# Squares of a weight behind the first cast of the weight before it, on ScalarE, in the first feed-forward half of a transformer block

## The chip, the cores and the metric

The kernel runs on one core of a Trainium2 chip. The metric is the device time of one execution in microseconds (us). Times named "of the profile" come from one execution that the hardware profiler recorded; the median comes from three other executions.

## The reference

One layer with a residual trunk, input x of 1 x 2048 x 1024 in float32:

```python
u2 = rms_norm(h, norm2_w[l])
gate = jnp.einsum('bsd,df->bsf', u2, w_gate[l])
up = jnp.einsum('bsd,df->bsf', u2, w_up[l])
h = h + jnp.einsum('bsf,fd->bsd', jax.nn.silu(gate) * up, w_down[l])
```

Ahead of this stands an attention part (an input projection, four heads of differential attention, eight heads of stick-breaking attention, an output projection) which the change does not touch. The hidden width is 2816.

## The kernel before, in words

**Arithmetic.** All large products run in float16 on TensorE, each operand as a high part and a low part (the high part is a cast, the low part is the rest), so that three float16 matmuls stand for one float32 matmul. A weight is scaled by a power of two ahead of the cast. The scale comes from the squares of the weight: a column sum over its squares, its maximum, and the exponent of that. On top of that the gate, up and down products use a scheme of seven products in place of eight on 2 x 2 blocks (`quad` and `down`). One `quad` issues seven groups of 12 matmuls, of 128 x 512 each, into the PSUM tiles `pa`, `pm`, `pm`, `pd`, and again `pa`, `pm`, `pd`. `pa` and `pd` are written twice: the second group adds to the bank, once VectorE or ScalarE has read the first result out of it.

**Stages.** The feed-forward part treats the 2048 rows in two halves. Each half runs over 11 steps of 256 hidden columns. A step has three weights of 128 x 2048 float32 values: g (gate), u (up) and d (down). In the first half each weight is loaded, scaled and split by `load_ffn`, used, and its seven split blocks are written to DRAM (`split`); the second half reads the split blocks back. Every step runs `gate` and then `up`; steps are collected in pairs, and the down products of a pair run in the next even step between its `gate` and its `up`. "Odd gate" and "even gate" are the gates of odd and even steps.

**The making of one weight (first half).** `stage` (L831) lets SyncE's queue load the weight into `fst`, which has two buffers. ScalarE squares it into `sq`, one buffer: L866 for g and u, and L184 in `scale_begin` for d, with the row sums along. TensorE adds the columns up into `fsc`: eight matmuls with ones for g and u (L874), one for d (L177). VectorE takes the maximum (L875, or L178 for d) and runs a chain of small operations (L195, L170, L171, L172, L130) to the scale `c` (L199). Then `split_weight` (L207) casts the blocks into `wg`, `wu` or `wd` on ScalarE (L210: two casts of 1024 values a partition, one from the small tile `sx` of 512, and one of 1024 behind GpSimd's work) and makes the low parts on VectorE (L215). GpSimd forms the sums and differences of blocks that the seven products need (L98, `fst<-fst` and `sx<-fst`). When all readers of an `fst` buffer are done, the next weight's transfer into it starts.

**The rest of the work around it.** The outputs of the gate products are emptied by ScalarE (L946) and VectorE (L949, L953, L959, L967, L970) into `cg` tiles, silu is applied on ScalarE (L981), VectorE multiplies by the up products (L998), and the activations are cast on ScalarE (L992) with their low parts on VectorE or GpSimd (L98). The down products L1034 are gathered by VectorE (L1040), with one copy on ScalarE (L1060).

**What sets the order.** Each engine runs its instructions in order. The program is written with generators: a weight's transfer and squares are issued at one place (`begin`), its scale and casts at a later one (`end`). Between them other work is written. A scheduler then decides the final order on each engine from its own estimate of the times, keeping data dependencies; `tc.issue_after(i)` tells it to issue what stands inside behind the instruction i. During the first two steps of the first half the kernel also finishes the normalised rows of the second half (`build_x`, tiles `bx`), and at the half's start the last output projections run (`po`, `wo`).

Of the kernel before, what the change touches and what calls it, by code (L numbers as in the profile page):

```python
# [15 lines left out]
AF = mybir.ActivationFunctionType  # L16
# [43 lines left out]
def block(tc, a, out):  # L60
    nc = tc.nc
    PE, ACT, DVE, POOL, SP = nc.tensor, nc.scalar, nc.vector, nc.gpsimd, nc.sync
    top = ExitStack()
    with top:
# [8 lines left out]
        def note(e, ns):  # L73
            load[e] += ns * KW[e]

        def pick(**cost):
            e = min(cost, key=lambda k: load[k] + cost[k] * KW[k])
            load[e] += cost[e] * KW[e]
            return e
# [29 lines left out]
        def nm(s):  # L109
            uid[0] += 1  # L110
            return f"{s}{uid[0]}"

        def c1(n=1, name="c"):
            t = cp.tile([P, n], F32, name=nm(name))
            return t
# [64 lines left out]
        def scale_begin(pieces, junk=None):  # L180
            m0 = sm.tile([P, 4], F32, tag="m0", name=nm("m0"))
            for j, pc in enumerate(pieces):
                if junk is not None:
                    ACT.activation(junk, pc, AF.Square, accum_out=m0[:, j : j + 1])  # L184
                    note("A", 0.84 * int(np.prod(pc.shape[1:])) + 200)
                else:
                    DVE.tensor_reduce(m0[:, j : j + 1], pc, op=ALU.max, axis=AX.XY if len(pc.shape) > 2 else AX.X, apply_absolute_value=True)
                    note("D", 1.05 * int(np.prod(pc.shape[1:])) + 100)
            return [m0[:, j : j + 1] for j in range(len(pieces))]
# [11 lines left out]
        def weight_scale(pieces, rW, pW, pt, junk=None):  # L201
# [2 lines left out]
            scale_end(lambda m: across(m, pt, cols), rW, pW, junk is not None, sW)  # L204
            return sW

        def split_weight(hi, lo, st, n, sW, engines="P"):  # L207
            e = pick(**{k: {"A": 0.84 * n + 200, "D": 0.53 * n + 130, "P": 1.1 * n + 100}[k] for k in engines})
            if e == "A":
                ACT.mul(hi, st, sW[:])  # L210
            elif e == "D":
                DVE.tensor_scalar(hi, st, sW[:], None, op0=ALU.mult)
            else:
                POOL.tensor_scalar(hi, st, sW[:], 0.0, op0=ALU.mult, op1=ALU.add)
            DVE.scalar_tensor_tensor(lo, st, sW[:], hi, op0=ALU.mult, op1=ALU.subtract)  # L215
            note("D", 1.05 * n + 130)
# [586 lines left out]
        with ExitStack() as ph2:  # L803
# [12 lines left out]
            def pst(t):  # L816
                pst_n[0] += 1
                if pst_n[0] % 4:
                    return ps2.tile([P, 512], F32, tag="b", bufs=6, name=nm(t))
                return psj.tile([P, 512], F32, tag="pj", name=nm(t))  # L820
# [6 lines left out]
            def stage(fg, nme):  # L827
                st = fw.tile([P, 2048], F32, tag="fst", bufs=2, name=nm("fst"))
                f0 = 256 * fg
                with tc.issue_after(rows[1].ins) if (fg, nme) == (1, "u") else nullcontext():  # L830
                    d = fetch(st, f0, nme)  # L831
                if len(keep) > 1:
                    with tc.issue_after(d.ins):
                        SP.dma_start(*keep.pop(0))
                return st
# [13 lines left out]
            def load_ffn(half, fg, names, W):  # L849
                eng = "ADP" if fg == 0 else WE  # L850
                sc = scales.setdefault(fg, {})
                for nme in names:
                    if half == 1:
                        yield
                        late = nme == "d" and fg == NFG - 1
                        w16 = (fd if nme == "d" and not late else fw).tile([P, 7, 2, 512], F16, tag="wd" if nme == "d" and not late else "wgu", bufs=2, name=nm("w" + nme))
                        SP.dma_start(w16[:].rearrange("p o s n -> p (o s n)"), split[fg, "gud".index(nme)])
                        W[nme] = w16
                        continue
                    st = stage(fg, nme)  # L860
                    r, p, sW = c1(), c1(), c1()
                    sq = fw.tile([P, 2048], BF16, tag="sq", bufs=1, name=nm("sq"))
                    if nme == "d":
                        cols = scale_begin([st[:]], sq[:])
                    else:
                        ACT.activation(sq[:], st[:], AF.Square)  # L866
                        note("A", 1900)
                    yield
                    w16 = (fd if nme == "d" else fw).tile([P, 7, 2, 512], F16, tag="wd" if nme == "d" else "wgu", bufs=2, name=nm("w" + nme))
                    pt = pst("fsc")  # L870

                    def columns(m):
                        for k in range(KT):
                            PE.matmul(pt[:, :256], lhsT=ones[:], rhs=sq[:, 256 * k : 256 * k + 256], start=k == 0, stop=k == KT - 1)  # L874
                        DVE.tensor_reduce(m, pt[:, :256], op=ALU.max, axis=AX.X)  # L875

                    scale_end((lambda m: across(m, pt, cols)) if nme == "d" else columns, r[:], p[:], True, sW)
                    sc[nme] = (r, p, sW)
                    sW = sc[nme][2]
                    tte = "DP" if fg == 0 else "P"  # L880
                    sx = fw.tile([P, 512], F32, tag="sx", bufs=1, name=nm("sx"))

                    def put(o, src, n):
                        split_weight(w16[:, o : o + n, 0], w16[:, o : o + n, 1], src, 512 * n, sW, eng)

                    if nme == "d":
                        sv = st[:].rearrange("p (f h n) -> p h f n", f=2, h=2)
                        b11, b21, b12, b22 = sv[:, 0, 0], sv[:, 0, 1], sv[:, 1, 0], sv[:, 1, 1]
                        put(0, sv[:, 0], 2)
                        tt(sx[:], b22, b12, ALU.subtract, 512, tte)  # L890
                        tt(b12, b12, b11, ALU.subtract, 512, tte)
                        tt(b11, b22, b12, ALU.subtract, 512, tte)
                        tt(b21, b21, b11, ALU.subtract, 512, tte)
                        put(2, sv[:, 1], 2)
                        put(4, sv[:, 0], 2)
                        put(6, sx[:].unsqueeze(1), 1)
                    else:
                        sv = st[:].rearrange("p (d k f n) -> p d k f n", d=2, k=4, f=2)
                        xv = sx[:].rearrange("p (k n) -> p k n", k=4)
                        wv = w16[:].rearrange("p o s (k n) -> p o s k n", k=4)  # L900

                        def putk(o, src, n):
                            split_weight(wv[:, o : o + n, 0], wv[:, o : o + n, 1], src, 512 * n, sW, eng)

                        blk = lambda f, d: sv[:, d, :, f, :]
                        putk(0, sv[:, :, :, 0, :], 2)
                        tt(xv, blk(0, 0), blk(1, 0), ALU.subtract, 512, tte)
                        tt(blk(1, 0), blk(1, 0), blk(1, 1), ALU.add, 512, tte)
                        tt(blk(0, 0), blk(1, 0), blk(0, 0), ALU.subtract, 512, tte)
                        tt(blk(0, 1), blk(0, 1), blk(0, 0), ALU.subtract, 512, tte)  # L910
                        putk(2, sv[:, :, :, 1, :], 2)
                        putk(4, sv[:, :, :, 0, :], 2)
                        putk(6, xv.unsqueeze(1), 1)
                    W[nme] = w16
                    keep.append((split[fg, "gud".index(nme)], w16[:].rearrange("p o s n -> p (o s n)")))
                    if fg == NFG - 1 and nme == "d":
                        while keep:
                            SP.dma_start(*keep.pop(0))
                if half == 0 and "g" in names:
                    kg, F = c1(), c1()  # L920
                    times(kg, sc["g"][1], p_2, 2.0 ** -14)
                    times(F, sc["g"][0], r_2, 2.0 ** (21 - 37))
                    sc["kg"], sc["F"] = kg, F
                if half == 0 and "d" in names:
                    kd = c1()
                    times(kd, sc["u"][1], p_2)
                    times(kd, kd, sc["d"][1])
                    times(kd, kd, sc["kg"], 2.0 ** (39 - 14 - 22))
                    sc["kd"] = kd
                W.update({k: sc[k] for k in ("kg", "F", "kd") if k in sc})  # L930
# [297 lines left out]
```

## Time and profile before

| what | us |
|---|---|
| median of three executions | 2779.86 (2775.68 to 2783.71) |
| span of the profiled execution | 2785.0 |
| first feed-forward half in it | about 1433 to 2105 |
| second feed-forward half in it | 2105 to 2785 |
| PE busy in the span | 2489.9 |
| DVE busy in the span | 2000.8 |
| POOL busy in the span | 1445.2 |
| ACT busy in the span | 1361.8 |

PE is TensorE's matmuls, DVE is VectorE, ACT is ScalarE, POOL is GpSimd, SP is SyncE, and SPq its DMA queue. A row of a timeline gives the start in the span, the duration of the run of like instructions in us, the engine, the line of the kernel, the operation, what is written and read with the shape, and the count; in brackets stands how long the engine idled before and what released it. A row of the waits gives the waiting instruction, whom it waited for, the total, the number of waits and the longest. A row of the windows gives the stretch, its length, the busy time of each engine with the number of instructions, the granted clock of TensorE as a share of full speed, the share of DMA time, and GB/s. Numbers behind tile names are left out there. In the listings of the order a tile's number is kept, and a row tells line, operation, output and inputs.

### The profile page before, as it was taken

The page shows a single profiled execution, that of the slowest core. Times are in us where ns is not written, and L with a number is a line of the kernel's source. Part 1 is how long each engine was busy: PE and PEld are TensorE (multiplying, and loading weights), DVE is VectorE, ACT ScalarE, POOL GpSimd, SP SyncE. Part 2 cuts the span into 40 slices and gives each one's busy share as a digit, 9 for nine tenths or more (in the row PEclk, how much of TensorE's full clock was granted, in tenths as well). Part 3 has the DMA queues.
Part 4 walks back from the last instruction along what each step waited for, and adds up shares of the span by engine and source line. Part 5 has one row for each costly group of instructions (what it writes and reads, how often), then busy time and mean ns, then how long its engine had stood idle before and what let it go on. Part 6 is the DMA issues. An engine that isn't in the chain of part 4 may idle for free. (4 is left out here: it accounts for less than half of the span.)

```text
span 2785.0 us, 45469 instructions
## 1 busy us (share of the span) xinstructions
PE 2489.9 (89%) x17084; PEld 1409.0 (51%) x17084; DVE 2000.8 (72%) x3782; ACT 1361.8 (49%) x2543; POOL 1445.2 (52%) x1008
## 2 busy tenths in 40 slices
PE   6998989888878786888889798989999999999998
PEld 4665556555545453557775343444444444444443
DVE  6888879687989989876756877777786644434445
ACT  4665656466878788765644534443442212111121
POOL 2567767665544555546665656565654332322323
PEclk9999999999999897999999999999999999999999
DMA  6788787789999998997796565655658844635534
GB/s 225 199 167 184 147 188 163 164 174 205 198 205 198 192 182 160 190 198 205 197 309 253 184 235 189 221 187 191 240 170 299 327 155 178 227 125 190 211 129 166
DMA packets 649133, 551.91 MB, mean 198 GB/s; under 512 B 506624, under 2 KB 574208, under 8 KB 638672
## 3 DMA queue, kind: packets, MB, share of 16 engines
q1 hardware_dynamic: 647088, 546.92, 71.2%
q8 instruction: 134, 2.20, 0.3%
q0 software_dynamic: 512, 1.36, 0.2%
q10 hardware_dynamic: 1312, 0.72, 0.1%
q14 instruction: 87, 0.71, 0.1%
HBM read 265.27 MB, written 151.52 MB: 150 GB/s over the span
## 5 line engine op out<-in xcount | busy, mean ns | idle before, releaser
L98 POOL TENSOR_TENSOR s<-z,s 128x1024 f16<-128x1024 f32 (+7 forms) x288 | 474.1, 1654 | 334.8 <-ACT s L89 299.3
L320 PE MATMUL pj<-w,xt 128*128 128x384 f16 x3072 | 572.3, 334 | 32.6 <-DVE st L330 11.6
L320 PEld LDWEIGHTS <-xt 128*128 128x128 f16 x3072 | 299.9, 100 | 241.8 <-issue 36.3
L448 PE MATMUL sc<-kT,qT 128*128 128x512 f16 (+3 forms) x1280 | 346.9, 362 | 74.6 <-DVE z L558 34.4
L1034 PE MATMUL pd<-wd,act 128*128 128x512 f16 x1848 | 406.2, 379 | 3.3 <-DVE hs L1040 2.4
L557 DVE TENSOR_TENSOR_SCAN z<-z,sc 128x512 f32<-128x512 f32 (+3 forms) x320 | 355.5, 1112 | 68.6 <-ACT sc L555 65.1
L458 PE MATMUL yp<-v,aT 128*128 128x64 f16 (+1 forms) x4896 | 281.2, 207 | 80.0 <-DMA aT<-s 79.2
L458 PEld LDWEIGHTS <-aT 128*128 128x128 f16 x4896 | 245.2, 102 | 169.4 <-DMA aT<-s 105.1
L936 PEld LDWEIGHTS <-wg 128*128 128x128 f16 x1848 | 183.9, 100 | 264.3 <-issue 58.8
L98 POOL TENSOR_TENSOR hs<-hs,cu 128x512 f32<-128x512 f32 x132 | 170.5, 1297 | 238.2 <-DVE cu L1040 82.6
L936 PEld LDWEIGHTS <-wu 128*128 128x128 f16 x1848 | 181.0, 98 | 222.1 <-issue 9.0
L1034 PEld LDWEIGHTS <-act 128*128 128x128 f16 x1848 | 180.6, 98 | 222.6 <-issue 4.7
L98 POOL TENSOR_TENSOR act<-cg,act 128x512 f16<-128x512 f32 x117 | 160.8, 1385 | 247.7 <-ACT act L992 141.5
L98 POOL TENSOR_TENSOR fst<-fst 128x512 f32<-128x512 f32 x97 | 179.6, 1852 | 167.6 <-DVE wd L215 78.6
L1040 DVE SCALAR_TENSOR_TENSOR hs<-pd,c,hs 128x512 f32<-128x512 f32 x192 | 142.1, 748 | 160.8 <-PE pd L1034 159.1
L89 ACT CAST s<-z 128x384 f16<-128x384 f32 (+7 forms) x216 | 170.1, 788 | 151.5 <-DMA aT<-s 56.4
L554 ACT ACTIVATE z<-sc,c 128x512 f32<-128x512 f32 (+3 forms) x320 | 202.6, 633 | 10.6 <-PE sc L448 6.5
L558 DVE TENSOR_TENSOR z<-sc,z 128x512 f32<-128x512 f32 (+3 forms) x320 | 193.3, 606 | 8.1
L992 ACT CAST act<-cg 128x512 f16<-128x512 f32 x132 | 80.6, 617 | 234.2 <-DVE cg L998 190.9
L555 ACT ACTIVATE sc<-sc,c 128x512 f32<-128x512 f32 (+3 forms) x320 | 194.8, 609 | 0.0
L761 PE MATMUL po<-wo,mt 128*128 128x256 f16 x1536 | 181.3, 276 | 11.0 <-DVE xf L764 6.3
L936 PE MATMUL pm<-X,wg 128*128 128x512 f16 x792 | 179.1, 379 | 1.2 <-ACT bx L1109 1.2
(233 smaller groups left out, 4028.4 us busy)
## 6 DMA issues: line engine op xcount, KB each, us to landing
xt<-xs SPq DMA_DIRECT2D x112, 512.0 KB, 4.4
hs<-hd SPq DMA_DIRECT2D x96, 512.0 KB, 4.3
hd<-hs SPq DMA_DIRECT2D x80, 512.0 KB, 3.2
split<-wg SPq DMA_DIRECT2D x11, 1792.0 KB, 10.5
split<-wu SPq DMA_DIRECT2D x11, 1792.0 KB, 10.3
split<-wd SPq DMA_DIRECT2D x11, 1792.0 KB, 10.4
wg<-split SPq DMA_DIRECT2D x11, 1792.0 KB, 7.3
wd<-split SPq DMA_DIRECT2D x11, 1792.0 KB, 8.4
```

Source lines behind the costliest of these rows:

```text
L89: ACT.copy(dst, src)
L98: (DVE if e == "D" else POOL).tensor_tensor(dst, a_, b_, op)
L320: PE.matmul(pj[:, :384], lhsT=xv[:, xi, kt, :], rhs=G["w"][:, wi, kt, :], start=n == 0, stop=n == 23)
L448: PE.matmul(sc[:, : 128 * w].rearrange("p (t n) -> p t n", n=P), lhsT=G["q"][i // 4][:, 2 - 2 * o + m, i % 4, :], rhs=G["k"][q][:, m, 0:w, ...
L458: PE.matmul(yp[:, y0 : y0 + wd], lhsT=aT[:, a_, :], rhs=v[:, v_ : v_ + wd], start=start and j == 0 and q == 0, stop=stop and j == nb - 1 a ...
L554: ACT.activation(om[:, lo:hi], sc[:, :w], AF.Sigmoid, scale=G["nkz"][:])
L555: ACT.activation(sc[:, :w], sc[:, :w], AF.Sigmoid, scale=G["kz"][:])
L557: DVE.tensor_tensor_scan(ov, ov, sc[:, :w], om[:, hi : hi + 1], op0=ALU.mult, op1=ALU.bypass)
L558: DVE.tensor_tensor(be[:, lo:hi], sc[:, :w], om[:, lo + 1 : hi + 1], ALU.mult)
L761: PE.matmul(po[:, sl], lhsT=mt[:, kt, P * xi : P * xi + P], rhs=wos[2 * h + n][wi][:, kt, :], start=q == 0, stop=q == 23)
L936: PE.matmul(ps_[:].rearrange("p (t n) -> p t n", n=P), lhsT=wv[:, wo, wi, 128 * kt : 128 * kt + 128], rhs=X[xo][:, :, xi, kt, :], start=st ...
L1034: PE.matmul(po[:], lhsT=act[:, ao, xi, 128 * j : 128 * j + 128], rhs=W["d"][:, wo, wi, :], start=start and u == 0 and q == 0, stop=u == nu ...
```

## The change

The ScalarE casts of a weight are kept in a list, which is emptied ahead of the next weight's casts. The squares of a weight are issued behind the first cast in the list, that is, behind the first ScalarE cast of the weight made before it. Nothing else is changed.

```diff
+        casts = []
+
+        def behind(k):
+            return tc.issue_after(casts[min(k, len(casts) - 1)].ins) if casts else nullcontext()
+
         def split_weight(hi, lo, st, n, sW, engines="P"):
             e = pick(**{k: {"A": 0.84 * n + 200, "D": 0.53 * n + 130, "P": 1.1 * n + 100}[k] for k in engines})
             if e == "A":
-                ACT.mul(hi, st, sW[:])
+                casts.append(ACT.mul(hi, st, sW[:]))
...
                     sq = fw.tile([P, 2048], BF16, tag="sq", bufs=1, name=nm("sq"))
-                    if nme == "d":
-                        cols = scale_begin([st[:]], sq[:])
-                    else:
-                        ACT.activation(sq[:], st[:], AF.Square)
-                        note("A", 1900)
+                    with behind(0):
+                        if nme == "d":
+                            cols = scale_begin([st[:]], sq[:])
+                        else:
+                            ACT.activation(sq[:], st[:], AF.Square)
+                            note("A", 1900)
...
                     sW = sc[nme][2]
                     tte = "DP" if fg == 0 else "P"
+                    casts.clear()
```

The scheduler decides the order of all engines anew under this condition. The two listings that differ most are shown at their places in the prediction.

## The prediction

> **What bounds the kernel now.** I read the page first, then the busy time by stage, then TensorE's waits in the stage that changes, then the timeline of one pair of steps there. From the page, the profiled time:
>
> ```profile
> span 2785.0 us, 45469 instructions
> ```
>
> The busy time by stage (PE's first, with its count, and the granted clock after the engines), two pairs of steps of the first feed-forward half and the whole second half:
>
> ```profile
> 1741.00:1869.00 128.00, 117.36 (x545) 54.19 (x543) 93.49 (x133) 52.85 (x62) 74.71 (x48) 0.96 0.58 201
> 1869.00:1997.00 128.00, 119.42 (x555) 55.10 (x553) 96.68 (x141) 55.50 (x65) 76.05 (x49) 0.97 0.59 205
> ...
> 2105.00:2785.00 680.00, 668.61 (x3094) 302.25 (x3091) 320.71 (x428) 119.90 (x188) 217.51 (x169) 1.00 0.54 201
> ```
>
> TensorE carries both halves. The second makes no weights and leaves nothing to gain; in the first TensorE misses 9 to 11 us in 128. Its waits in the first half (us in total, times, longest):
>
> ```profile
> PE pd L936 <- DVE cg L959: 30.4, 8, 5.9
> PE fsc L874 <- ACT sq L866: 9.2, 6, 2.4
> PE pa L936 <- ACT cg L946: 6.4, 2, 3.3
> ```
>
> One pair of steps on TensorE:
>
> ```profile
> 1799.37 4.44 PE L936 MATMUL pd<-X,wg 128*128 128x512 f16 x12 [3.47 <-DVE cg L959]
> 1803.64 0.71 PE L874 MATMUL fsc<-sq,ones 128*128 128x256 bf16 x5
> ...
> 1811.95 0.38 PE L177 MATMUL fsc<-id,m 128*128 128x128 f32 x2
> 1812.17 2.75 PE L936 MATMUL pd<-X,wu 128*128 128x512 f16 x12
> ...
> 1827.81 1.03 PE L874 MATMUL fsc<-sq,ones 128*128 128x256 bf16 x8 [1.26 <-ACT sq L866]
> ...
> 1847.25 4.73 PE L936 MATMUL pd<-X,wg 128*128 128x512 f16 x12 [5.89 <-DVE cg L959]
> ```
>
> Three holes: A, in the odd gate; B, where the even gate needs the column sums of u; C, late in the even gate, where VectorE has not emptied a bank. Behind A and C the twelve matmuls last 4.4 to 4.7 instead of 2.75 us. Why VectorE is late at C is seen some 35 us earlier. ScalarE, then VectorE:
>
> ```profile
> 1807.75 1.91 ACT L184 ACTIVATE sq<-fst 128x2048 bf16<-128x2048 f32 x1 [5.26 <-DMA fst<-in_w_down_dram]
> ...
> 1809.66 0.71 ACT L981 ACTIVATE cg<-cg,c 128x512 f32<-128x512 f32 x1
> 1810.28 2.17 ACT L210 ACTIVATE wg<-fst,c 128x1024 f16<-128x1024 f32 x2
> 1812.35 0.71 ACT L210 ACTIVATE wg<-sx,c 128x512 f16<-128x512 f32 x1
> ...
> 1825.85 1.91 ACT L866 ACTIVATE sq<-fst 128x2048 bf16<-128x2048 f32 x1 [1.07 <-DMA fst<-in_w_up_dram]
> ```
>
> ```profile
> 1805.65 0.15 DVE L199 TENSOR_SCALAR c<-c 128x1 f32<-128x1 f32 x1
> ...
> 1811.44 2.48 DVE L215 SCALAR_TENSOR_TENSOR wg<-fst,c,wg 128x1024 f16<-128x1024 f32 x2 [5.52 <-ACT wg L210]
> ...
> 1831.66 2.17 DVE L215 SCALAR_TENSOR_TENSOR wd<-fst,c,wd 128x1024 f16<-128x1024 f32 x1
> ...
> 1846.52 0.68 DVE L959 TENSOR_TENSOR cg<-pd,cg 128x512 f32<-128x512 f32 x1
> ```
>
> The scale of g is there at 1805.80, yet its casts start at 1810.28: in front of them on ScalarE stand d's squares, which wait for d's weight, and a silu behind those. VectorE, which makes the low parts, idles 5.52 us, then has work without a long wait until 1846.52. u's buffer is the one that g frees, so u's transfer, u's squares and hole B hang on the same delay.
>
> **The change: d's squares.** No instruction is added or removed. ScalarE at that place, before (sq_22378 are d's squares, wg_22338 the casts of g, cg silus, cu the up product):
>
> ```order
> L981 ACTIVATE cg_22269<-cg_22269,c_21901 128x512
> L184 ACTIVATE sq_22378,m_22379<-fst_22372 128x2048
> L981 ACTIVATE cg_22240<-cg_22240,c_21901 128x512
> L210 ACTIVATE wg_22338<-fst_22271,c_22276 128x2x512 x2
> L210 ACTIVATE wg_22338<-sx_22355,c_22276 128x512
> L946 COPY cu_22395<-pa_22382 128x512
> ```
>
> and with the change (line numbers stand 5 to 7 higher):
>
> ```order
> L988 ACTIVATE cg_22269<-cg_22269,c_21901 128x512
> L988 ACTIVATE cg_22240<-cg_22240,c_21901 128x512
> L215 ACTIVATE wg_22338<-fst_22271,c_22276 128x2x512 x2
> L215 ACTIVATE wg_22338<-sx_22355,c_22276 128x512
> L184 ACTIVATE sq_22378,m_22379<-fst_22372 128x2048
> L953 COPY cu_22395<-pa_22382 128x512
> ```
>
> The squares moved behind three casts. The casts can start at about 1805.9, 4.4 us earlier. VectorE's low parts, GpSimd's subtractions that follow them, the release of g's buffer and so u's transfer move with them, and C's add comes at about 1842.1. u's squares, 4.4 earlier, are done at 1823.4 against 1827.8: hole B closes. d's squares start at 1805.9 + 2.17 + 0.71, about 1808.7 (their data were there at 1807.75), and end 1810.7; TensorE asks for their maximum at 1811.95. Cover 1.3 us, cost 0. (In the middle pairs like that of 1966 the new order puts this matmul one product later on TensorE, with more cover.) The third cast of g keeps waiting for GpSimd's subtractions, only earlier, and d's and u's casts follow suit.
>
> **Hole A.** VectorE there, before, and then with the change (cg the odd gate, wu_22197 the odd u's low parts, act an activation's):
>
> ```order
> L949 TENSOR_TENSOR cg_22240<-pm_22242,cg_22240 128x512
> L98 TENSOR_TENSOR act_22040<-cg_21672,act_22040 128x512
> L215 SCALAR_TENSOR_TENSOR wu_22197<-fst_22112,c_22117,wu_22197 128x2x512
> L953 TENSOR_TENSOR cg_22269<-pm_22256,cg_22240 128x512
> L215 SCALAR_TENSOR_TENSOR wu_22197<-fst_22112,c_22117,wu_22197 128x2x512
> L215 SCALAR_TENSOR_TENSOR wu_22197<-sx_22214,c_22117,wu_22197 128x512
> L964 TENSOR_TENSOR cg_22292<-pd_22279,cg_22269 128x512
> ```
>
> ```order
> L98 TENSOR_TENSOR act_22040<-cg_21672,act_22040 128x512
> L956 TENSOR_TENSOR cg_22240<-pm_22242,cg_22240 128x512
> L220 SCALAR_TENSOR_TENSOR wu_22197<-fst_22112,c_22117,wu_22197 128x2x512 x2
> L960 TENSOR_TENSOR cg_22269<-pm_22256,cg_22240 128x512
> L220 SCALAR_TENSOR_TENSOR wu_22197<-sx_22214,c_22117,wu_22197 128x512
> L966 TENSOR_TENSOR cg_22292<-pd_22279,cg_22269 128x512
> ```
>
> The same set stands ahead of the last add, so A stays. One add now runs behind the wait for `act` instead of ahead of it: between 0 and one add (0.68), I take 0.3. Besides, all eight column sums of g now run behind the gate's `pd`, where before three ran ahead of it in the hole: 1.03 less 0.71, 0.3. A costs 0.6 a pair, and delays g's scale by as much.
>
> **The squares elsewhere.** In the odd step, u's squares go behind d's casts, and in the down products d's go behind the next g's:
>
> ```profile
> 1869.13 1.91 ACT L184 ACTIVATE sq<-fst 128x2048 bf16<-128x2048 f32 x1 [8.01 <-PE fsc L874]
> ...
> 1887.50 1.91 ACT L866 ACTIVATE sq<-fst 128x2048 bf16<-128x2048 f32 x1 [8.25 <-DMA fst<-in_w_up_dram]
> ...
> 1898.14 2.19 ACT L210 ACTIVATE wd<-fst,c 128x1024 f16<-128x1024 f32 x2 [6.41 <-DVE c L199]
> ```
>
> ```profile
> 1896.07 0.39 PE L177 MATMUL fsc<-id,m 128*128 128x128 f32 x2
> ...
> 1906.65 1.04 PE L874 MATMUL fsc<-sq,ones 128*128 128x256 bf16 x8
> ```
>
> u's squares would end at 1898.14 + 2.19 + 0.71 + 1.91, about 1902.9, and their sums are taken at 1906.65: cost 0, 3.7 us of cover. d's squares, now at 1869.13, move by the 2.9 us of three casts, and TensorE takes their maximum at 1896.07: cost 0; the down products' own copy on ScalarE (L1060) behind them comes at most the 1.4 us later that a scale needs from its sums (1804.35 to 1805.80), less than the one product that TensorE has in hand there: cost 0. Should a cover fail, each us beyond it is one us of TensorE.
>
> **First and last pair.** Other holes, on TensorE, and the ScalarE rows of the first pair:
>
> ```profile
> 1454.86 2.78 PE L761 MATMUL po<-wo,mt 128*128 128x256 f16 x24 [1.76 <-DVE wo L764]
> ...
> 1555.81 0.49 PE L177 MATMUL fsc<-id,m 128*128 128x128 f32 x2 [1.99 <-ACT sq L184]
> ...
> 1573.36 1.03 PE L874 MATMUL fsc<-sq,ones 128*128 128x256 bf16 x8 [1.76 <-ACT sq L866]
> ...
> 1593.21 5.28 PE L936 MATMUL pd<-X,wg 128*128 128x512 f16 x12 [5.01 <-DVE cg L959]
> ...
> 1713.99 4.44 PE L936 MATMUL pa<-X,wg 128*128 128x512 f16 x12 [3.26 <-ACT cg L946]
> ...
> 1966.79 4.44 PE L936 MATMUL pa<-X,wg 128*128 128x512 f16 x12 [3.18 <-ACT cg L946]
> ...
> 2079.88 1.03 PE L874 MATMUL fsc<-sq,ones 128*128 128x256 bf16 x8 [1.20 <-ACT sq L866]
> ...
> 2097.67 4.12 PE L936 MATMUL pd<-X,wg 128*128 128x512 f16 x12 [4.45 <-DVE cg L959]
> ```
>
> ```profile
> 1553.77 1.89 ACT L184 ACTIVATE sq<-fst 128x2048 bf16<-128x2048 f32 x1
> ...
> 1555.66 2.17 ACT L210 ACTIVATE wg<-fst,c 128x1024 f16<-128x1024 f32 x2
> ```
>
> In the first pair d's squares ran at once, so the casts gain only 1.9 us, and TensorE waits 2.9 us more for the maximum of d (1.99 now), which the 1.76 of B and C's 5.01 take up. I take 2.5, between 0 and 6. In the last pair the new order puts three low parts ahead of C's add; I take 2, between 0 (all of the 4.4 lost) and 4.4. At the start u's squares go behind two casts of g, about 1.8 us, while TensorE projects outputs (half of 2.17 and 0.71); the hole at 1454.86 and smaller ones take up most: a cost of 0.5, between 0 and 1.8.
>
> **Sum.** Three full middle pairs at 4.4 - 0.6 = 3.8: 11.4. First 2.5, last 2, start -0.5: 15.4, call it 15. The span goes from 2785.0 to about 2770. That execution is 5 us above the median shown, 2779.86, so the forecast on the median is 2765. About 0.3%, 8 us, is what a measurement here can tell from nothing.
>
> **Rivals.** *More gain.* C's wait shrinks from 5.89 to 5.89 + 1.26 - 4.4, about 2.8 us. Whether the twelve matmuls behind it stay slow is open:
>
> ```profile
> 1672.43 2.75 PE L936 MATMUL pd<-X,wg 128*128 128x512 f16 x12 [2.65 <-DVE cg L959]
> ```
>
> ```profile
> 1672.40:1675.20 2.80, 2.77 (x14) 1.34 (x14) 1.09 (x1) 2.27 (x3) 2.72 (x3) 1.00 0.00 0
> ...
> 1847.20:1852.00 4.80, 4.75 (x13) 1.72 (x13) 2.36 (x2) 2.05 (x4) 2.88 (x2) 0.57 0.40 73
> ```
>
> A wait of 2.65 left the clock at 1.00; 3.26 and 5.89 cost it (4.44 and 4.73, clock 0.57 in the latter). If all five C holes end below, 2.53 + 1.7 + 2.0 + 1.7 + 1.4 us are saved besides, 9: 2756. The Trainium skill (TensorE: Matmul & The Clock Gate, Part 1) halves the clock after an idle window of about 3.4 us that runs freely; by that limit alone all shortened C holes would stay at full clock. The trace agrees only in kind: a hole of 3.26 was already slow. Chance 0.1.
>
> *No change.* The gain is lost on VectorE. Two low parts of g take 2.48 together now, while one of d takes 2.17. If moving them puts GpSimd beside all three of g's, each costs 0.9 more, 2.7 a pair, and with A's 0.6 the pairs keep 1.1: 3 in the middle, 2 at the ends, 2775. The Trainium skill (SBUF — State Buffer, section SBUF: two separate sides) has such an operation fully block, not slow down in part. Against: GpSimd's work on g starts only behind g's first low part, so the block moves as a whole. Chance 0.2, with the lesser losses of this sign.
>
> *Slower.* d's squares behind the casts come too late for TensorE, which stops in order at their maximum. It decides at 1.3 us: if g's casts start more than that behind 1805.9. If they started as late as now, the squares would end at about 1815.2 and TensorE wait 3.2 us; at three pairs that is 10, with A's 3 and the start, 14: 2794. Against: the silus and the scale ahead of the casts are done by 1805.9 in the trace. That the order of a schedule differs from what I replay by hand is the main doubt. Chance 0.12.
>
> **Numbers.** Forecast as summed 0.58, more 0.1, no change 0.2, slower 0.12. Faster by over 0.3%: 0.68. The range goes from somewhat past the larger gain, 2753, to the upper edge of no change, 2779, and leaves out the slower case.
>
> **What would show it.** Right: VectorE's 5.5 us idle before g's low parts shrinks below 2; the six waits of the column sums for u's squares (9.2) nearly vanish; `pd` for `cg` L966 falls from 30.4 to about 22; A keeps its 3 us. Wrong: a wait of `fsc` L177 for the squares of d at every even gate, or C's waits unchanged with longer low parts.

## The result

| kernel | median us | ratio to before, 95% interval |
|---|---|---|
| before | 2781.78 (2775.68 to 2784.83, 4 runs) | |
| with the change | 2755.95 (2754.82 to 2757.25, 4 runs) | 0.991 (0.9894 to 0.9926) |
| with the change, built and timed again (the last experiment) | 2759.37 (2754.36 to 2764.57, 5 runs) | 0.9918 (0.9904 to 0.9933) |

The change saves 21 to 26 us, each median against the kernel before on the same chip (2781.78, and 2780.83 for the second timing). The forecast was 15 us, 2765 in a range from 2753 to 2779. The change is faster and the time inside the range, but the gain is 1.4 to 1.7 times the forecast, close to the price that the prediction had given to its rival of a larger gain (2756).

### The profile after

TensorE's waits in the first feed-forward half, after, in the view that was shown of before (line numbers are 7 higher here, 5 in the weight's helper):

```profile
span 2754.1 us, 45485 instructions
```

```profile
PE pd L943 <- DVE cg L966: 23.1, 9, 4.4
PE fsc L177 <- ACT sq L184: 7.0, 2, 6.7
PE fsc L880 <- ACT sq L872: 3.0, 2, 2.3
...
PE pa L943 <- ACT cg L953: 1.7, 2, 1.6
```

The total of the whole list falls from 63 to 42 us. The wait for the column sums of u and g went from 9.2 to 3.0, `pd` for `cg` from 30.4 to 23.1, and `pa` for ScalarE's copy from 6.4 to 1.7. One wait grew by more than 0.2 us, from 2.5 to 7.0: that for the maximum of d, nearly all of it at one place in the first pair.

The same pair of steps as in the prediction, after:

```profile
1778.47 2.75 PE L943 MATMUL pd<-X,wg 128*128 128x512 f16 x12 [1.62 <-DVE cg L966]
1781.05 1.04 PE L880 MATMUL fsc<-sq,ones 128*128 128x256 bf16 x8
...
1790.15 0.49 PE L177 MATMUL fsc<-id,m 128*128 128x128 f32 x2 [0.29 <-ACT sq L184]
...
1803.21 1.04 PE L880 MATMUL fsc<-sq,ones 128*128 128x256 bf16 x8
...
1822.27 5.28 PE L943 MATMUL pd<-X,wg 128*128 128x512 f16 x12 [4.42 <-DVE cg L966]
```

A fell from 3.47 to 1.62 us and has fast matmuls behind it, B is closed, and C fell from 5.89 only to 4.42. ScalarE, then VectorE, where the casts of g start:

```profile
1783.99 2.19 ACT L215 ACTIVATE wg<-fst,c 128x1024 f16<-128x1024 f32 x2 [0.59 <-issue]
1786.09 0.71 ACT L215 ACTIVATE wg<-sx,c 128x512 f16<-128x512 f32 x1
1788.10 1.91 ACT L184 ACTIVATE sq<-fst 128x2048 bf16<-128x2048 f32 x1 [1.30 <-DMA fst<-in_w_down_dram]
...
1790.01 0.56 ACT L953 COPY cu<-pa 128x512 f32<-128x512 f32 x1
```

```profile
1783.76 0.15 DVE L199 TENSOR_SCALAR c<-c 128x1 f32<-128x1 f32 x1
...
1785.18 2.48 DVE L220 SCALAR_TENSOR_TENSOR wg<-fst,c,wg 128x1024 f16<-128x1024 f32 x2 [1.14 <-ACT wg L215]
...
1790.61 0.69 DVE L956 TENSOR_TENSOR cu<-pm,cu 128x512 f32<-128x512 f32 x1 [1.27 <-ACT cu L953]
```

The casts start as soon as the scale is there, and VectorE's 5.52 us of idle time are 1.14. But d's squares still wait for their transfer, now with ScalarE's copy of the up product queued behind them, and VectorE waits 1.27 us for that copy. That is a new wait; the experiment with d and g below shows that it is the main part of what C did not lose.

### Where the 30.9 us between the two profiled spans are

The two profiles are apart before the changed part begins. An issue on SyncE's queue just ahead of it, in the kernel before, with the change, and with the change in a second profile:

```profile
1425.71 0.87 SPq L766 DMA_DIRECT2D hd<-xf  x1
```

```profile
1419.36 0.86 SPq L771 DMA_DIRECT2D hd<-xf  x1
```

```profile
1427.89 0.87 SPq L771 DMA_DIRECT2D hd<-xf  x1
```

Up to there all three have the same instruction lists. Two profiles of one and the same kernel differ by 8.5 us, so the 6 us here are scatter between executions and are no part of the change. Hence the times below are taken inside the first half, from the first matmul of the up product of step 0 to that of step 10:

| kernel | step 0 to 10, us | first pair | pairs at steps 4, 6, 8 | last pair |
|---|---|---|---|---|
| before | 638.7 | 135.5 | 126.3, 127.7, 125.1 | 124.0 |
| with the change | 614.5 | 131.2 | 118.6, 122.2, 120.4 | 122.1 |
| with the change, second profile | 613.0 | 129.9 | 118.6, 122.1, 120.4 | 122.0 |

24 and 26 us, about what the medians say: 4 to 6 in the first pair, 7.7, 5.5 and 4.7 in the middle pairs (a pair is named by its even step), 2 in the last. From step 10 to the end both spans last 648.8 us, so nothing of the change lies there.

### The profile page after: what moved, and what is told of

It is laid out like the page before. It is cut to its first block, busy times and chain, and to the rows that moved or that the text cites. A ratio compares the mean times of both kernels' runs of the same rounds, so it can differ in the third digit from the quotient of the medians.

```text
span 2754.1 us, 45485 instructions
## 1 busy us (share of the span) xinstructions
PE 2491.4 (90%) x17084; PEld 1411.9 (51%) x17084; DVE 1997.4 (73%) x3782; ACT 1361.3 (49%) x2543; POOL 1447.6 (53%) x1008
## 5 line engine op out<-in xcount | busy, mean ns | idle before, releaser
L98 POOL TENSOR_TENSOR act<-cg,act 128x512 f16<-128x512 f32 x117 | 166.6, 1437 | 231.4 <-ACT act L999 125.1
## 6 DMA issues: line engine op xcount, KB each, us to landing
split<-wg SPq DMA_DIRECT2D x11, 1792.0 KB, 11.4
split<-wd SPq DMA_DIRECT2D x11, 1792.0 KB, 10.5
```

Source lines behind the costliest of these rows:

```text
L98: (DVE if e == "D" else POOL).tensor_tensor(dst, a_, b_, op)
```

## The experiments

The theories in the expectations: theory 1 is the prediction's (d's squares delay g's casts, and so VectorE). Theory 2 came from the two profiles: g's squares, which stood ahead of ScalarE's copy and casts in the odd gate, were what made A long. All kernels start from the changed kernel. A third buffer for the weights, which would take the wait for the transfer away by itself, was not tried.

| run | median us | ratio to before, 95% interval | steps 0 to 10, us |
|---|---|---|---|
| d alone | 2761.38 | 0.9925 (0.9910 to 0.9940) | 616.8 |
| g alone | 2773.95 | 0.9971 (0.9960 to 0.9983) | 626.0 |
| u alone | 2784.07 | 1.0006 (0.9994 to 1.0018) | 640.8 |
| all but the d of step 1 | 2765.53 | 0.9937 (0.9922 to 0.9953) | 618.8 |
| all but that d and the u of step 2 | 2764.28 | 0.9936 (0.9924 to 0.9949) | 619.4 |
| d of odd steps alone | 2761.80 | 0.9926 (0.9915 to 0.9938) | 616.3 |
| all, low parts of activations on GpSimd | 2753.16 | 0.9899 (0.9883 to 0.9915) | 611.9 |
| all, VectorE slowed ahead of C | 2764.48 | 0.9934 (0.9922 to 0.9947) | 617.6 |
| d and g | 2762.85 | 0.9926 (0.9911 to 0.9941) | 616.0 |
| all, block sums shared with GpSimd | 2776.81 | 0.9978 (0.9967 to 0.9989) | 629.1 |
| d and g, low parts on GpSimd | 2754.50 | 0.9892 (0.9873 to 0.9912) | 611.8 |

### One weight's squares at a time

```diff
-                    with behind(0):
+                    with behind(0) if nme == "d" else nullcontext():
```

> Only d's squares go behind the casts of the weight before; g's and u's squares stay where they were. Theory 1 (the prediction's: the gain comes from d's squares letting VectorE start g's low parts 4.4 us earlier in the even gates): nearly all of the 26 us of the full change, 22 to 27, so 2755 to 2760 beside a kernel before at about 2781; the holes A in the odd gate stay as they were with the full change. Theory 2 (from the two traces: g's squares standing ahead of ScalarE's copy and casts were what made A as long as it was): 15 to 20 us, so 2761 to 2767, with VectorE's idle before g's low parts gone but A at 2.6 to 3.5 us again.

Measured: 21 us faster, between the two forecasts of the gain (22 to 27 and 15 to 20); the interval, 17 to 25 us, does not tell them apart. The holes do: A is 2.66, 3.50, 2.98 and 2.75 us at steps 4 to 10, as before the change and as theory 2 has it, not as with the full change. So d's squares bring most of the gain and leave A alone. VectorE's waits for g's casts behind 1600 us, before and with d alone (us, times, longest), show the mechanism:

```profile
DVE wg L215 <- ACT wg L210: 27.4, 11, 7.6
```

```profile
DVE wg L220 <- ACT wg L215: 6.5, 7, 1.1
```

And the holes A and C of the pair at step 6, with d alone:

```profile
1790.05 4.16 PE L943 MATMUL pd<-X,wg 128*128 128x512 f16 x12 [3.50 <-DVE cg L966]
1833.40 4.44 PE L943 MATMUL pd<-X,wg 128*128 128x512 f16 x12 [3.03 <-DVE cg L966]
```

A stays at 3.5, B is gone, and C falls from 5.89 to 3.03, near the 2.8 us that the prediction had for it.

```diff
+                    with behind(0) if nme == "g" else nullcontext():
```

> Only g's squares go behind the casts of the weight before. Theory 1: no gain or a loss of up to 3 us (0.6 a pair): 2781 to 2784. Theory 2: the holes A fall to about 1.5 us in two of the five pairs and by 0.2 to 0.4 in two more, with one slow group of matmuls (1.7 us) gone: 4 to 9 us, so 2772 to 2777, while VectorE still idles about 5 us before g's low parts and C stays.

Measured: 9 us faster, as theory 2 says. VectorE's wait for g's casts stays (27.1 us in 11 waits), and A shrinks to 1.26 and 1.39 us at steps 4 and 6; at steps 8 and 10 it hardly moves (2.88 and 2.90). At step 6, with g alone:

```profile
1787.39 2.75 PE L943 MATMUL pd<-X,wg 128*128 128x512 f16 x12 [1.39 <-DVE cg L966]
...
1835.39 3.09 PE L943 MATMUL pd<-X,wg 128*128 128x512 f16 x9 [3.13 <-DVE cg L966]
```

Theory 2 missed one thing: C at step 6 did not stay, it fell from 5.89 to 3.13 us. But B grew there from 1.26 to 2.29, and a wait of 1.52 us for a scale is new, so the time went to other holes, and the fall of C alone is no sign of d's squares. The reason for the shorter A is visible in the rows of before. ScalarE, then VectorE, ahead of A:

```profile
1787.77 1.91 ACT L866 ACTIVATE sq<-fst 128x2048 bf16<-128x2048 f32 x1 [1.04 <-DMA fst<-in_w_gate_dram]
1789.59 0.57 ACT L946 COPY cg<-pa 128x512 f32<-128x512 f32 x1
```

```profile
1789.22 0.15 DVE L199 TENSOR_SCALAR c<-c 128x1 f32<-128x1 f32 x1
1790.18 0.69 DVE L949 TENSOR_TENSOR cg<-pm,cg 128x512 f32<-128x512 f32 x1 [0.82 <-ACT cg L946]
1791.74 0.71 DVE L98 TENSOR_TENSOR act<-cg,act 128x512 f16<-128x512 f32 x1 [0.87 <-ACT act L992]
1792.79 1.76 DVE L215 SCALAR_TENSOR_TENSOR wu<-fst,c,wu 128x1024 f16<-128x1024 f32 x1 [0.34 <-ACT wu L210]
...
1798.63 0.68 DVE L959 TENSOR_TENSOR cg<-pd,cg 128x512 f32<-128x512 f32 x1
```

and after, VectorE at the same place:

```profile
1771.68 0.14 DVE L199 TENSOR_SCALAR c<-c 128x1 f32<-128x1 f32 x1
1772.26 0.88 DVE L98 TENSOR_TENSOR act<-cg,act 128x512 f16<-128x512 f32 x1 [0.43 <-ACT act L999]
...
1773.66 2.46 DVE L220 SCALAR_TENSOR_TENSOR wu<-fst,c,wu 128x1024 f16<-128x1024 f32 x2
...
1776.65 1.16 DVE L220 SCALAR_TENSOR_TENSOR wu<-sx,c,wu 128x512 f16<-128x512 f32 x1
1777.73 0.68 DVE L966 TENSOR_TENSOR cg<-pd,cg 128x512 f32<-128x512 f32 x1
```

Before, g's squares waited for their transfer and held up the copy and the casts behind them, and VectorE idled 0.82 + 0.87 + 0.34 us. After, 0.43. The low parts took 1.76, 1.97 and 1.75 us before and 2.46 for two and 1.16 for the third after. From the scale to A's last add it is 9.4 us before (1789.22 to 1798.63) and 6.05 after: 3.4 us less.

```diff
+                    with behind(0) if nme == "u" else nullcontext():
```

> Only u's squares go behind the casts of the weight before. Theories 1 and 2 agree: these squares have 3.7 us of cover in the odd steps and stand behind their own transfer in the even ones: within 2 us of the kernel before, about 2780. A rival (u's squares are what closes hole B) would have B's waits of 1.2 to 2.4 us gone and 6 to 9 us gained.

Measured: no difference. With u alone the column sums still wait 10.5 us in seven places, while with d alone, where u's squares were not moved, B is gone in all pairs from step 4 on. What moves with d is u's transfer: counted from the start of the up product of step 5, it is issued after 15.1 us before, 15.0 with u alone and 10.7 with d alone. So B closes through the earlier transfer of u, not through the place of its squares.

### d and g together

```diff
+                    with behind(0) if nme != "u" else nullcontext():
```

> The full change without u: d's and g's squares go behind the casts, u's stay. d alone gave 21.3 us, g alone 8.7, u alone -1.4 (within its interval of nothing). Theory 2 with parts that add up: 28 to 30 us faster than the kernel before, 2752 to 2755, the same as the full change (25.8) within 3. Rival (u's squares are needed once the others move): 2762 or slower, as both kernels that kept some of u's or d's squares in the first pair.

Measured: 20 us faster, so the parts do not add up (21 and 9 alone), and the time cannot be told apart from that of d alone, nor from the full change. The pair at step 6, with d and g:

```profile
1784.61 2.75 PE L943 MATMUL pd<-X,wg 128*128 128x512 f16 x12 [1.40 <-DVE cg L966]
...
1828.43 5.28 PE L943 MATMUL pd<-X,wg 128*128 128x512 f16 x12 [4.49 <-DVE cg L966]
```

Against d alone, A is 2.1 us shorter and its matmuls are 1.4 faster, but C is 1.5 longer and its matmuls 0.8 slower. Where C's 1.5 us come from stands on ScalarE and VectorE behind g's casts, with d alone and then with d and g; the last row of each is C's add:

```profile
1798.99 1.89 ACT L184 ACTIVATE sq<-fst 128x2048 bf16<-128x2048 f32 x1
...
1801.55 0.68 DVE L956 TENSOR_TENSOR cu<-pm,cu 128x512 f32<-128x512 f32 x1
...
1832.67 0.68 DVE L966 TENSOR_TENSOR cg<-pd,cg 128x512 f32<-128x512 f32 x1
```

```profile
1794.19 1.91 ACT L184 ACTIVATE sq<-fst 128x2048 bf16<-128x2048 f32 x1 [1.25 <-DMA fst<-in_w_down_dram]
...
1796.70 0.69 DVE L956 TENSOR_TENSOR cu<-pm,cu 128x512 f32<-128x512 f32 x1 [1.22 <-ACT cu L953]
...
1827.70 0.68 DVE L966 TENSOR_TENSOR cg<-pd,cg 128x512 f32<-128x512 f32 x1
```

Counted from the start of the up product of step 5 (1794.59 and 1788.07), TensorE is ready for C after 35.8 and 35.9 us, but VectorE's first add of the up product starts after 7.0 and 8.6, and C's add after 38.1 and 39.6. A shorter A brings all of this forward, except d's transfer: it was issued 2.7 us ahead of that start with d alone and 0.5 with d and g. So d's squares wait for it, ScalarE's copy waits behind them, and VectorE behind the copy. Theory 2 explains A, and A is worth little once d's squares are moved. That u's squares are needed once the others move, as the rival says, is not shown, though the time is the rival's: the pairs of d and g and of the full change differ clearly only at step 4 (120.4 and 118.6 us), where the matmuls behind C are slow in one and fast in the other, and with all low parts of activations on GpSimd steps 0 to 10 take 611.8 us without u and 611.9 with it.

### Down products, first pair

```diff
+                    with behind(0) if nme == "d" and fg % 2 else nullcontext():
```

> Only the squares of d of odd steps go behind g's casts; these are the ones that stand in an even gate. The d's of even steps, in the down products, stay where they were, and so do g's and u's squares. Theory 1 and 2 agree, and the prediction's zero for the down products: the same as when all d's move, 2761 within 3 us. Rival (the d's in the down products bring part of it): 2765 to 2772.

Measured: 2761.80 beside 2761.38. The zero for d's squares in the down products holds.

```diff
+                    with behind(0) if (fg, nme) != (1, "d") else nullcontext():
```

> The full change, but the squares of the d of step 1 (first pair) stay where they were. With the full change TensorE waits 6.66 us for the maximum of this d, 1.99 before, and the next twelve matmuls take 5.23 instead of 2.75 us. Theory 2: that wait falls back to about 2 and the slow group goes, 7 us, of which the later waits (C of this pair, 1.29 now, 5.01 before; B) take back 4 to 5: 2 to 3 us faster than the full change, about 2753. Rival: C takes all of it back, since g's casts start behind the squares again, and the time is 2756 to 2758.

Measured: steps 0 to 10 take 4 to 6 us longer than with the full change. TensorE's wait for that maximum did fall, from 6.66 to 1.76, but C of that pair, with the change and without this one move, is

```profile
1583.99 2.75 PE L943 MATMUL pd<-X,wg 128*128 128x512 f16 x12 [1.29 <-DVE cg L966]
```

```profile
1585.06 5.28 PE L943 MATMUL pd<-X,wg 128*128 128x512 f16 x12 [5.70 <-DVE cg L966]
```

The rival was right and too mild: C took 4.4 of the 4.9 us back, the slow matmuls behind the one hole now stand behind the other, and two smaller waits (1.64 for the up product, 1.21 at B) are new. The hole at the maximum of d had not been a loss of its own; it stood in for C.

```diff
+                    with behind(0) if (fg, nme) not in ((1, "d"), (2, "u")) else nullcontext():
```

> The full change, but in the first pair the squares of d (step 1) and of u (step 2) stay where they were. In the traces the first pair lasts 135.5 us before, 131.2 with the full change, 133.5 with the full change but for that d, and 128.3 when only g's squares move. Theory 2 (each square's move is priced by the holes around it, pair by pair): the first pair as with g alone, the rest as with the full change: 131.2 - 128.3, about 3 us faster than the full change, 2751 to 2754. Rival (the orders of neighbouring pairs hang together, so that pairs can't be added): 2756 or slower.

Measured: 2764.28, no better, with the same 5.70 us at C. In the run with g alone, C of that pair is 2.81 us; the scheduler had set VectorE's list there in another order. The rival holds: pairs cannot be put together from kernels whose lists were decided apart.

### VectorE's list ahead of the holes

```diff
-LE, SE, AE = "DP", "D", "P"
+LE, SE, AE = "P", "D", "P"
```

> The full change, and all low parts of activations on GpSimd (before 15 of the 77 in each half or so on VectorE, one of them right ahead of the last add of hole A). Theory 2 (A and C end when VectorE's list is worked off): A falls by the 0.9 to 1.2 us of that low part in the pairs, and the two A holes of 2.7 us that were followed by slow matmuls end below, 1.7 us more each: 5 to 9 us faster than the full change, 2747 to 2751. Rival (GpSimd, with the weight's subtractions queued behind more work, becomes the bound of the third casts): 2756 or slower.

Measured: 2753.16, ratio 0.9899, beside 0.991 and 0.9918 of the full change: perhaps 3 us, within the intervals, and not the 5 to 9 that theory 2 had. A at step 8 did fall from 2.68 to 2.05, yet its matmuls stayed slow, and at step 4 A rose from 1.45 to 2.06.

```diff
+                if tag == "cg" and now[0] == 0 and now[1] % 2 == 0 and now[1]:
+                    for _ in range(2):
+                        DVE.tensor_tensor(u3[:], u3[:], u3[:], ALU.max)
                 c22 = cst()
```

> The full change, with two more VectorE operations (maximum of a tile with itself, 0.6 us each, no change to the values) ahead of hole C's last add in the five even gates of the first half. If C is bound by VectorE at all five: 5 times 1.2, 6 us, and two C holes (2.44 and 2.65 now, at full clock behind them) grow beyond 3 us, which in every row so far cost 1.4 to 1.9 us more: 9 us in all, 2763 to 2767. If C were bound by something else (ScalarE's copy, GpSimd): 2756 to 2759. If the clock did not hang on the hole's length: 2762.

Measured: 2764.48, at the forecast for a C bound by VectorE. All five C holes grew, by 6.2 us together: that of step 4 from 2.44 to 3.43 us, that of step 8 from 2.65 to 3.63, that of step 6 from 4.42 to 5.75. Steps 0 to 10 grew by only 3 to 5 us, in part since the matmuls behind two A holes of 2.69 us, slow with the full change, were fast here. The part on the clock half fell: the two C holes that were to grow beyond 3 us are

```profile
1706.29 4.19 PE L943 MATMUL pd<-X,wg 128*128 128x512 f16 x12 [3.43 <-DVE cg L971]
```

```profile
1949.89 2.75 PE L943 MATMUL pd<-X,wg 128*128 128x512 f16 x12 [3.63 <-DVE cg L971]
```

the shorter with slow matmuls behind it, the longer with fast ones.

```diff
-LE, SE, AE = "DP", "D", "P"
+LE, SE, AE = "DP", "DP", "P"
```

> The full change, and the sums of activation blocks (always on VectorE) may go to GpSimd where it has less work: 11 of them move, of about 1.3 us each on VectorE. Theory 2 (the remaining C holes, 1.3 to 4.4 us, last as long as VectorE's list): those in the first half fall by up to 1.3 us each, 3 to 6 us faster than the full change. Rival (GpSimd's longer chain, or the clock behind holes of 2 to 3 us, takes it back): 2754 to 2760.

Measured: steps 0 to 10 take 15 to 16 us longer than with the full change. The balance of the kernel's own costs gave the sums to GpSimd and, in return, three activation low parts to VectorE, in a row right ahead of A's last add:

```profile
1791.62 3.63 DVE L98 TENSOR_TENSOR act<-cg,act 128x512 f16<-128x512 f32 x3
1795.17 0.68 DVE L966 TENSOR_TENSOR cg<-pd,cg 128x512 f32<-128x512 f32 x1
```

A at step 6 is 4.50 us there, 1.62 with the full change. So it did not test what it was meant to (a shorter list), only that what stands right ahead of that add counts.

```diff
-LE, SE, AE = "DP", "D", "P"
+LE, SE, AE = "P", "D", "P"
...
+                    with behind(0) if nme != "u" else nullcontext():
```

> d's and g's squares moved, u's not, and all low parts of activations on GpSimd. If parts add up: the gain of d and g (28 to 30) and the 3 us of the low parts: 2749 to 2752, the fastest kernel here. Rival: 2753 or slower, since the holes that shrink stay between 1.9 and 3.1 us, where the matmuls behind them were slow about every second time.

Measured: 2754.50, ratio 0.9892, at the rival's forecast. It is the lowest ratio of the study, but its interval (0.9873 to 0.9912) holds the ratio of all squares with the low parts on GpSimd (0.9899) and the first of the full change (0.9910). A kernel that beats the changed one was not shown.

### The full change a second time

> The full change once more, unaltered, for a second profiled execution of the same instruction lists. In the ten profiles so far the matmuls behind a hole were at full clock below 1.9 us, slow above 4, and either in between. If between 1.9 and 3.1 us it is chance (where the hole falls in a window of its own), the holes have the same lengths within 0.1 us, but of the four of 2.4 to 2.7 us (two slow in the first profile) another set is slow; if it is fixed by the work around the hole, the same two are slow. The 5.5 us by which the first profile was ahead of that of the kernel before by 1425 us, where both have the same lists, is scatter if it differs here by over 2 us. Time: 2754 to 2759.

Measured: 2759.37. From the pair at step 4 on the holes are the same within 0.1 us; in the first pair three differ (2.40 and 0.72, 2.31 and 3.14, and 6.66 and 4.13 for the maximum of d). The lead of the first profile ahead of the changed part was scatter. A and C at step 8 in both profiles, first and second:

```profile
1901.74 4.44 PE L943 MATMUL pd<-X,wg 128*128 128x512 f16 x12 [2.68 <-DVE cg L966]
...
1945.24 2.75 PE L943 MATMUL pd<-X,wg 128*128 128x512 f16 x12 [2.65 <-DVE cg L966]
```

```profile
1910.56 4.44 PE L943 MATMUL pd<-X,wg 128*128 128x512 f16 x12 [2.69 <-DVE cg L966]
...
1954.05 2.75 PE L943 MATMUL pd<-X,wg 128*128 128x512 f16 x12 [2.64 <-DVE cg L966]
```

A is slow and C fast in both. So it is with the other two of the four holes of 2.4 to 2.7 us, A at step 10 (2.69 and 2.68, slow) and C at step 4 (2.44, fast). That speaks for the work around a hole and against chance, in two executions.

## Why the prediction came out as it did

**d's squares: right, and the main term.** They alone give 21 of the 21 to 26 us. VectorE's idle time went as forecast (5.52 to 1.14), u's transfer came 4.4 us earlier with d alone, B closed.

**The sum: inside its range in part by luck, since its terms were wrong.** What TensorE lost less in the three middle pairs (at steps 4, 6 and 8), in us against before, worked out from the same rows in each profile:

| | forecast | d alone | g alone | d and g | full change |
|---|---|---|---|---|---|
| holes B and C | 13.2 | 9.6 | 0.8 | 6.6 | 7.0 |
| hole A (forecast with its column sums) | -1.8 | 0.0 | 3.6 | 3.6 | 3.4 |
| other waits | 0 | 2.4 | -1.4 | 2.2 | 2.1 |
| busy time | 0 | 3.1 | 2.8 | 3.3 | 5.3 |
| all | 11.4 | 15.2 | 5.9 | 15.7 | 17.8 |

The main term, 4.4 us a pair in B and C, was half as large in the full change. It was taken over from the pair at step 6, where d alone gives 4.1; at steps 4 and 8 it gives 2.9 and 2.7, since C there was a wait of `pa` for ScalarE's copy before and is one of `pd` for VectorE after. What made up for it the prediction had at nothing: at step 4, waits of TensorE for d's and the up product's values (0.51, 0.69 and 1.21 us before) went as well; and of the busy time, 4.4 us are faster matmuls behind A and C, 1.7 of them at C of step 4 and 1.7 at C of step 8.

**A: wrong in sign.** "The same set stands ahead of the last add, so A stays" counted VectorE's instructions, and not its waits between them, 2 us of which were for ScalarE's copy and casts behind g's squares, nor how long the low parts take at their new place. (The last row of the prediction's first listing there is L959 in the kernel before.) A fell by 1.2, 1.9, 0.4 and 0.2 us at steps 4, 6, 8 and 10. But the experiment with d and g shows that most of that comes back at C.

**d's squares' cover of 1.3 us: just used up.** TensorE waits 0.29 us at step 6. The squares end later than replayed since their transfer, not the casts, is what they wait for. The copy that is queued behind them, which the prediction quoted as the row below without pricing it, makes VectorE wait 1.27 us. With d alone neither of the two waits is there and C is 3.03 us; with d and g both are, and C is 4.49. So this chain accounts for C at step 6 being 4.42 and not 2.8; no run moved the copy alone.

**First pair, last pair, start.** Forecast 2.5, 2 and -0.5; measured 4.3 and 5.6 in two profiles, 2, and nothing that can be told. The wait for the maximum of d was put at 1.99 + 2.9, and is 6.66 and 4.13 in two profiles. At the start the holes between the output projections shrank (1.76, 1.13, 0.91 and 0.50 before; 1.20, 0.67 and 0.70 after, one of them now at the column sums), but from one and the same matmul there to the up product of step 0 it is 72.4 us before, and 71.2 and 73.0 in two profiles after.

**The rivals.** More gain: the total is what it named, 2756, and only partly for its reason. The slow groups behind holes in the half cost about 15 us before and 11 to 12 after, so the clock gave 3 to 4 us, not 9, and the waits the rest. No change through longer low parts: the three of g took 1.28, 1.28 and 1.76 us at step 6, as before, and only the fourth grew, from 1.28 to 1.91. Slower through d's squares: it happens in the first pair, where the wait grew by up to 4.7 us, and C's fall from 5.01 to 1.29 pays for most of it.

## What to carry to other kernels

An engine that works in order should not have an instruction that waits for a transfer ahead of work whose inputs are there: look at what idles downstream of it, here VectorE 35 us ahead of TensorE's hole. Holes that are ends of one engine's list are not separate gains, so price them together; shortening one moves time to the next, and taking one away by hand can cost more than it was. And count the waits inside a list, not only its instructions.

## What the hardware showed

In 14 profiles, the 157 holes of at least 1 us ahead of gate and up matmuls in the first half were followed by slow matmuls (12 in 4.0 to 5.3 us instead of 2.75) as follows: under 1.9 us 1 of 37, from 1.9 to 3.1 us 43 of 72, from 3.1 to 4 us 27 of 29, above 4 us all 19. The granted clock behind the hole of 4.42 us is 0.50, that behind the one of 2.65 us 1.00:

```profile
1822.30:1827.30 5.00, 5.00 (x12) 1.74 (x12) 2.35 (x2) 2.02 (x3) 2.79 (x2) 0.50 0.41 96
1945.30:1948.00 2.70, 2.70 (x13) 1.21 (x13) 2.32 (x2) 1.63 (x3) 2.62 (x2) 1.00 0.00 0
```

The length of a hole does not decide alone, and neither chance nor a cause was found for the rest: one kernel repeated its slow holes, while C holes of 2.63 to 2.66 us at step 8 were slow in three kernels and fast in five, and A holes of 2.69 us were slow with the full change and fast where VectorE was slowed. The Trainium skill (TensorE: Matmul & The Clock Gate, Part 1) has the clock halve after about 3.4 us of idle time, in a window that runs freely; the halved clock agrees, the 43 slow holes below 3.1 us do not agree with that length as a limit, and the freely running window would fit holes of one length that differ, though not two executions that agree.

Two profiles of one kernel were 8.5 us apart after 1420 us of the same instruction lists. A comparison of two spans is then no measure of a change of 10 us; a stretch between two marks inside the changed part is.
